# An fp32 encoder layer on one Trainium2 core: attention packed into fewer ticks, operand sets built earlier, and a reordered beginning

## The chip, the cores and the metric

The kernel runs on one core of a Trainium2 chip. The metric is the device time of one launch in microseconds (us), as the median of several runs. One more execution was recorded by the hardware profiler. TensorE is PE in its rows (PEld: its weight loads), VectorE is DVE, ScalarE is ACT, GpSimd is POOL and SyncE is SP.

## The reference

One layer over 768 tokens (a prompt of 256 and a sample of 512 are two segments that share the weights), all in float32:

```python
ada = jax.nn.silu(c) @ w_ada + b_ada
shift, scl, gate = jnp.split(ada, 3, axis=-1)
h = _rms(x, norm_g) * (1 + scl[:, None, :]) + shift[:, None, :]
proj = h @ w_in                                   # 2048 -> 10240
pool_u, pool_z, q, k, v, attn_z, g_pool, g_attn = jnp.split(proj, cuts, axis=-1)
pool_y = _pool_mixer(pool_u, pool_w, pool_scale) * jax.nn.silu(pool_z)
...                                               # q and k are normalised per head
attn_y = _neighbourhood_attention(q, k, v, rpb) * jax.nn.silu(attn_z)
merged = jax.nn.sigmoid(g_pool) * (pool_y @ w_pool_up) + jax.nn.sigmoid(g_attn) * (attn_y @ w_attn_up)
return x + gate[:, None, :] * (merged @ w_o)
```

Attention has 16 heads of 64 channels; each token attends to a window of up to 8 rows of 16 columns on a grid 64 wide, with a learned position bias.

## The kernel before

Every engine's instructions are written out in order by one generator (`steps`), so an engine waits wherever its next instruction is not ready. Activations lie as channels x tokens, 128 channels by 768 tokens in two halves of 384 (`TH`). Each large product is made of float32 split into a high and a low fp32r part, three matmuls of 128 x 128 by 384 columns for one block.

The matrix products come in sets, one per left operand: XA (channels 0 to 1023 of the normalised input, against w_in), XB (channels 1024 to 2047), XR (the pooled branch, against w_pool_up), XY (the attended branch, against w_attn_up), MA and MB (the halves of the merged branches, against w_o). Each set has an *opening* of two plain units (96 matmuls, L458) and then *pair jobs* (L440): two blocks of output at a time, by a Strassen-like scheme with seven products over four pairs of channels, 84 matmuls. The program counts in *ticks*: six matmuls each, 14 to a job, 16 to an opening. ScalarE and VectorE split the weights (`whi` at L329, `wlo` at L330) and combine the products (L368 copies one to `u` or `p`).

A set's operands are B11, B12, B21, B22 and the differences T1 to T4, each for four pairs. `Set.put` makes one: ScalarE casts the high part (L194), VectorE subtracts it for the low part (L198); the differences are formed at L218 to L230. `build` lists this work as tasks: fetch a pair (two loads of 384 KB), put its four blocks, make its T's. `whole=n` finishes the first n pairs, T's and all, before the next pair is fetched; the other pairs get their T's after all blocks. `pump` does at most one task in a tick, in an opening one each tick, in pair jobs one every second or third, and only if the buffers not in use exceed the task's need by `spare` (`SLOTS` is 45). When PE comes to an operand that is not there, `need` does all tasks up to it at once, in haste:

```python
def need(st, op, j):
    hurry["on"] = True
    while (op, j) not in st.ops:
        ...
        tasks.pop(0)[2]()
```

Beginning. SP loads 16 tiles of the input (`xin`), five tiles of the modulation weights (`adaw`, five buffers), four units of w_in (`wraw`), then the other `adaw`. ScalarE squares each `xin` tile, VectorE adds the squares (L1031), PE sums them over channels (`ss`, L1036). Then come the modulation's multiplications (`adaacc`, L477) in four groups of 16 steps, with opening ticks of XA in between (first main matmul: L458).

Attention is spread over XB's jobs, one job's matmuls between its pieces: `attention(p, start, pace)` puts unit u's stages at ticks start + pace x u + d. Of a unit's stages on PE, the scores `s` (L568) come at d = 0, the transposes `vt` of V (L607) at 5, the transposes `pt` of the probabilities (L629) at 9, the products `op` with V (L662) at 13. `vt` and `pt` share one PSUM tag; VectorE frees it by writing the low part `pl` (L647). `n2` (the norms of q and k, L503) and `yk` (L539) come once a head. Each head takes the time of 56 ticks: four jobs.

The branch gates are loaded ahead by `sig_load`.

Of the kernel before, what the change touches and what calls it, by code (L numbers as in the profile page):

```python
# [51 lines left out]
def encoder_layer(ctx: ExitStack, tc: tile.TileContext, xT, cT, w_ada2, w_ada4, b_ada, norm_g, w_in, pool_w,  # L52
# [22 lines left out]
    def free(n=1):  # L75
        heap["live"] -= n
# [219 lines left out]
    st_ = {"ahead": 3, "loaded": 0, "split": 0, "raw_live": 0}  # L296
# [190 lines left out]
    def norms(p, start):  # L487
# [11 lines left out]
        def sums():  # L499
            n2 = ps_aux.tile([P, 512], F32, tag="pt", name="n2")  # L500
# [267 lines left out]
    def store_part(f):  # L768
        def go(i, t):
            pool.dma_start(part_d[f], flat(t))  # L770
            after(3, free)
        return go

    def merge_part(f):
        def go(i, t):
            pool.dma_start(part_d[f], flat(t), accum_op=ALU.add)
            after(3, free)
        return go
# [82 lines left out]
    GR = (3, 2, 1, 0)  # L861

# [16 lines left out]
    for p in range(8):  # L879
# [20 lines left out]
    def pu_done(f):  # L900
        def go(i, t):
# [5 lines left out]
            sig_load(f + 4)  # L907
        return go

    def au_done(f):  # L910
        def go(i, t):
# [3 lines left out]
            if 16 + f + 4 < 32:  # L915
                sig_load(16 + f + 4)
# [84 lines left out]
    with tc.tile_pool(name="start", bufs=1) as sp_:  # L1001
# [21 lines left out]
        load_more()  # L1023
        acc = slot("sumsq")
        for kt in range(KT):
            if kt == 0:
                act.activation(flat(acc), flat(xin[kt]), AF.Square)
            else:
                sq = slot("sq0")
                act.activation(flat(sq), flat(xin[kt]), AF.Square)  # L1030
                dve.tensor_tensor(flat(acc), flat(acc), flat(sq), op=ALU.add)  # L1031
                free()
        free(8)
        ss = ps_aux.tile([P, 2, 512], F32, tag="s", name="ss")
        for h in range(2):
            pe.matmul(ss[:, h, :TH], ones, acc[:, h, :], start=True, stop=True)  # L1036
# [28 lines left out]
        for g, (inner, tail) in enumerate(PLAN):  # L1065
            adaw["acc"] = ps_aux.tile([P, 512], F32, tag="pt", name="adaacc")
            done = 0
            for kt in range(KT):
                ada_mm(adaw["acc"], kt, adaw[g, kt // 2][:, 512 * (kt % 2) : 512 * (kt % 2) + 512])
                if kt % 2:  # L1070
                    load_ada()
# [6 lines left out]
            if g == 0:  # L1078
                prepare(3)
# [9 lines left out]
        ready = {"pairs": 0}  # L1089
# [18 lines left out]
        def late_out(g):  # L1108
            tr = turned(4)
            if g < 2:  # L1110
                modulation(4 + g, tr)
                ready["pairs"] = 2 * g + 2
# [24 lines left out]
        early = started + 14 * len(jobsA) - 100  # L1137
        heap["spare"] = 4
        build(XB, x_pair, lambda j: j < ready["pairs"] and clock["now"] >= early, x_make, 0, 1)
        run(14 * len(jobsA))  # L1140


    with tc.tile_pool(name="mixp", bufs=1, reuse_waits="tile") as mp_:
# [5 lines left out]
        run(1)  # L1149
        free()  # L1150
        run(16 + 8 * 14 + 4 * 4 - 1)
# [23 lines left out]
    with tc.tile_pool(name="attn", bufs=1, reuse_waits="tile") as at_:  # L1175
        state["pool"] = at_
        act.preload_act_table_set(LNEXP)
        now = clock["now"]
        for p in range(8):
            attention(p, now + 56 * p + 25, 8)  # L1180
        run(31 * 14 - 40)
        build(XR, pooled)
        build(XY, attended, lambda j: state.get("attended", -1) >= 2 * j + 1, gated, 2, 1)
        run(40)
        for f in range(4):
            sig_load(f)
        run(16 + 2 * 14)
# [98 lines left out]
```

## Time and profile before

| | us |
|---|---|
| median of 3 runs | 2068.19 |
| lowest and highest | 2067.04, 2069.83 |
| the profiled execution | 2067.87 |
| its span in the trace | 2066.1 |
| PE busy, of the span | 1949.3 |
| DVE, ACT, POOL busy | 1332.6, 1025.3, 259.6 |

The profiled execution is the time of the launch in which the trace was taken; the span is what the trace covers of it. Busy times of engines overlap. A busy PE need not be at full speed: the clock granted to it stands beside it in the views by stretch, 1.00 for the higher of its two levels.

### The profile page before, as it was taken

The numbers are of one execution on the slowest core, as the hardware profiler recorded it, in microseconds if no ns is written. First come the engines' busy times: TensorE is split into PE (matmuls) and PEld (weight loads), VectorE is DVE, ScalarE is ACT, GpSimd is POOL, SyncE is SP. The second block draws the span as 40 slices with busy tenths as digits, with TensorE's granted clock in tenths as the row PEclk, the third lists the DMA queues.
The fourth block names the chain that finished last, engine by engine and source line by source line (L and its number), as shares of the span: only waits on it lengthen the run. The fifth ranks groups of instructions, "written<-read, shape, count | busy, mean of one in ns | idle before, by whom it ended". The sixth has DMA issues, their size and how long they took to land.

```text
span 2066.1 us, 31567 instructions
## 1 busy us (share of the span) xinstructions
PE 1949.3 (94%) x11812; PEld 1834.4 (89%) x11812; DVE 1332.6 (64%) x2392; ACT 1025.3 (50%) x2207; POOL 259.6 (13%) x385
## 2 busy tenths in 40 slices
PE   3899999999999989999999999999979979999998
PEld 2889898888999879999999999999968968999997
DVE  5755555555566777756667666666766767677654
ACT  4433333333344344546556556556656555456653
POOL 0000000000000045410000100101100001112111
PEclk9999999999999989999999999999979999999999
DMA  9755555553333425555545545445634647767765
GB/s 354 258 189 182 200 189 202 191 189 138 136 138 134 154 57 143 133 126 119 126 97 127 119 105 127 109 115 125 172 119 151 246 157 191 226 162 197 207 174 142
DMA packets 100362, 331.92 MB, mean 161 GB/s; under 512 B 13169, under 2 KB 18289, under 8 KB 100209
## 3 DMA queue, kind: packets, MB, share of 16 engines
q1 hardware_dynamic: 68256, 217.35, 30.9%
q0 software_dynamic: 30944, 112.48, 23.4%
q8 instruction: 92, 1.51, 0.3%
q14 instruction: 62, 0.50, 0.1%
q10 hardware_dynamic: 1008, 0.09, 0.0%
HBM read 251.22 MB, written 78.64 MB: 160 GB/s over the span
## 4 chain that ended last, share of the span: by engine, by line
PE 81%; DVE 6%; ACT 5%; DMA 4%; issue 3%; POOL 0%; SPq 0%; ACTq 0%; POOLq 0%; DVEq 0%
PE acc L440 71%; PE acc L458 2%; PE adaacc L477 2%; PE op L662 1%; DMA adaw<-in_w_ada_dram 1%; DVE wlo L330 1%; ACT whi L329 1%; PE s L568 1%; PE n L503 1%; PE pt L629 1%; DMA wraw<-in_w_in_dram 1%; DVE sumsq L1031 1%; PE yk L539 1%; DMA in<-pooled_d 0%; DMA in<-merged_d 0%
## 5 line engine op out<-in xcount | busy, mean ns | idle before, releaser
L330 DVE TENSOR_TENSOR wlo<-wraw,whi 128x512 fp32r<-128x512 f32 (+1 forms) x357 | 249.1, 699 | 296.6 <-ACT whi L329 283.7
L330 DVE TENSOR_TENSOR wlo<-wsum,whi 128x512 fp32r<-128x512 f32 x420 | 293.6, 699 | 132.5 <-ACT whi L329 130.9
L440 PE MATMUL acc<-xbT,whi 128*128 128x384 f32 x1248 | 339.9, 353 | 10.5 <-DVE xbT L198 5.2
L329 ACT CAST whi<-wsum 128x512 fp32r<-128x512 f32 x420 | 260.6, 621 | 160.0 <-ACT whi L329 49.5
L440 PE MATMUL acc<-xaT,whi 128*128 128x384 f32 x1216 | 313.7, 338 | 1.1 <-ACT u L368 0.6
L329 ACT CAST whi<-wraw 128x512 fp32r<-128x512 f32 (+1 forms) x357 | 215.8, 605 | 116.1 <-PE acc L440 92.8
L368 ACT COPY u<-acc 128x384 f32<-128x384 f32 x210 | 100.5, 478 | 300.5 <-PE acc L440 300.5
L440 PE MATMUL acc<-xbB,whi 128*128 128x384 f32 x936 | 247.3, 345 | 0.5 <-DVE o L757 0.5
L440 PEld LDWEIGHTS acc<-xbT,whi 128*128 128x128 f32 x1248 | 229.9, 196 | 20.1 <-DVE xbT L198 7.4
L440 PE MATMUL acc<-xaB,whi 128*128 128x384 f32 x912 | 235.4, 339 | 0.0
L440 PEld LDWEIGHTS acc<-xaT,whi 128*128 128x128 f32 x1216 | 217.6, 188 | 16.2 <-issue 14.4
L440 PE MATMUL acc<-xbT,wlo 128*128 128x384 f32 x624 | 215.3, 345 | 0.0
L440 PE MATMUL acc<-xaT,wlo 128*128 128x384 f32 x608 | 203.9, 335 | 0.0
L440 PEld LDWEIGHTS acc<-xaB,whi 128*128 128x128 f32 x912 | 163.0, 188 | 11.9 <-issue 9.9
L440 PEld LDWEIGHTS acc<-xbB,whi 128*128 128x128 f32 x936 | 167.4, 191 | 4.4 <-issue 1.4
L440 PE MATMUL acc<-xbB,wlo 128*128 128x384 f32 x468 | 158.1, 338 | 0.0
L353 DVE TENSOR_TENSOR wsum<-wraw 128x512 f32<-128x512 f32 x210 | 145.4, 693 | 13.4 <-DMA wraw<-in_w_in_dram 13.2
L440 PE MATMUL acc<-xaB,wlo 128*128 128x384 f32 x456 | 153.0, 335 | 0.0
L353 DVE TENSOR_TENSOR wsum<-wsum,wraw 128x512 f32<-128x512 f32 x210 | 147.5, 702 | 0.0
L440 PEld LDWEIGHTS acc<-xbT,wlo 128*128 128x128 f32 x624 | 121.8, 195 | 0.0
L440 PEld LDWEIGHTS acc<-xaT,wlo 128*128 128x128 f32 x608 | 114.2, 188 | 0.0
L379 DVE SCALAR_TENSOR_TENSOR o<-u,acc 128x384 f32<-128x384 f32 x105 | 58.2, 554 | 85.8 <-ACT u L368 83.8
(252 smaller groups left out, 3435.9 us busy)
## 6 DMA issues: line engine op xcount, KB each, us to landing
wraw<-in_w_in_dram SPq DMA_DIRECT2D x160, 512.0 KB, 4.4
adaw<-in_w_ada_dram SPq DMA_DIRECT2D x96, 512.0 KB, 5.4
part_d<-o POOLq DMA_DIRECT2D x116, 384.0 KB, 2.8
wraw<-in_w_o_dram SPq DMA_DIRECT2D x32, 512.0 KB, 6.4
o<-part_d POOLq DMA_DIRECT2D x38, 384.0 KB, 4.8
sig<-part_d SPq DMA_DIRECT2D x32, 384.0 KB, 7.0
wraw<-in_w_pu_dram SPq DMA_DIRECT2D x16, 512.0 KB, 4.5
wraw<-in_w_au_dram SPq DMA_DIRECT2D x16, 512.0 KB, 5.9
```

Source lines behind the costliest of these rows:

```text
L329: act.copy(hi[:, :n, :], raw)
L330: dve.tensor_tensor(lo[:, :n, :], raw, hi[:, :n, :].bitcast(F32), op=ALU.subtract)
L353: dve.tensor_tensor(t[:, :n, :], a, b, op=ALU.add)
L368: act.copy(t, c["a"][:, :TH])
L379: dve.scalar_tensor_tensor(c["o2"][:, 1, :], c["u3"], -1.0, c["c"][:, :TH], op0=ALU.mult, op1=ALU.subtract)
L440: pe.matmul(out, w, m, start=s["first"] and j == 0 and k == 0, stop=j == n - 1 and k == 2, skip_group_check=True)
L458: pe.matmul(c["ps"][h], w[:, j, :], mov[h][m], start=s["begin"] and j == 0 and k == 0, stop=last and k == 2, skip_group_check=True)
L477: pe.matmul(acc[32 * j : 32 * (j + 1), :n], cs[:, kt, :], w[:, n * j : n * (j + 1)], start=kt == 0, stop=kt == KT - 1)
L503: pe.matmul(n2[:, 12 * i + 2 * u : 12 * i + 2 * u + 2], flat(c["s" + nm])[:, P * u : P * (u + 1)], blk1[:, 0:P:64], start=True, stop=True)
L539: pe.matmul(c["b"][HALF[h], u // 3, P * (u % 3) : P * (u % 3 + 1)], src, ident, start=True, stop=True)
L568: pe.matmul(s[:, h, :K], a[HALF[h], q0 : q0 + P], b[HALF[h], key0 : key0 + K], start=i == 0, stop=i == 2)
L629: pe.transpose(pt[:n, j, h, :], c["p"][:, h, o_ : o_ + n], ident)
```

## The change

The change has five parts.

1. *Beginning.* The squares of odd `xin` tiles are summed by PE as they come, into the same `ss`; VectorE adds only the even ones. Ten of group 0's 16 modulation steps stand on PE ahead of the last sum. The first three units of w_in load two of their eight channel blocks at first; the rest, and the fourth unit, are loaded after group 0's modulation.
2. *XB's building.* XA's last part writes its outputs into a pool of its own (`outs_a`, seven buffers). XB is built with `whole=2` and `spare` 1, from 110 ticks before the end of XA's jobs instead of 100, and no longer waits for pairs to be modulated.
3. *Attention.* Five heads (`DENSE`) lie over 42 ticks instead of 56, at pace 7 instead of 8; the five jobs that stood in them follow after the last head. `n2` moves from the PSUM tag that `pt` and `vt` share to that of the scores.
4. *XR and XY* are built after attention has ended, with the pool `outs`, XR with `whole=2`. By the program's count XR's opening begins at tick 1142; pair 1 is fetched at 1137, pairs 2 and 3 at 1150. For XY pair 1 is fetched at 1203 (before: 1240), pair 2 at 1240 (1246), pair 3 at 1255 (1259); its T's still come partly in haste. MA's pairs 2 and 3 are fetched four ticks earlier. XB's pairs 2 and 3 are fetched at ticks 555 and 557; its opening begins at 564.
5. *Gates* are loaded two ahead instead of four.

```diff
     def load_more():
-        while st_["loaded"] < len(units) and st_["raw_live"] < RAWBUFS:
+        while st_["loaded"] < min(len(units), st_["upto"]) and st_["raw_live"] < RAWBUFS:
...
-            sp.dma_start(u["tile"][:, : u["n"], :], u["src"])
+            n = 2 if st_["loaded"] < st_["cut"] else u["n"]
+            sp.dma_start(u["tile"][:, :n, :], u["src"][:, :n, :])
...
+    def load_rest():
+        for u in units[: st_["cut"]]:
+            sp.dma_start(u["tile"][:, 2 : u["n"], :], u["src"][:, 2 : u["n"], :])
+        st_["upto"] = len(units)
...
-            n2 = ps_aux.tile([P, 512], F32, tag="pt", name="n2")
+            n2 = ps_aux.tile([P, 2, 512], F32, tag="s", name="n2")[:, 0, :]
...
+    DENSE = 5
...
-        for _ in range(2):
+        for _ in range(1 if p < DENSE else 2):
             a, b = gs.pop(0), gs.pop(0)
             jobs.append((a, b, fill(a), fill(b)))
+    while gs:
+        a, b = gs.pop(0), gs.pop(0)
+        jobs.append((a, b, fill(a), fill(b)))
...
-            sig_load(f + 4)
+            sig_load(f + 2)
...
         for kt in range(KT):
-            if kt == 0:
-                act.activation(flat(acc), flat(xin[kt]), AF.Square)
-            else:
-                sq = slot("sq0")
-                act.activation(flat(sq), flat(xin[kt]), AF.Square)
+            sq = acc if kt == 0 else slot("sq0")
+            act.activation(flat(sq), flat(xin[kt]), AF.Square)
+            if kt % 2:
+                summed(sq, kt == 1, False)
+            elif kt:
                 dve.tensor_tensor(flat(acc), flat(acc), flat(sq), op=ALU.add)
...
-        for h in range(2):
-            pe.matmul(ss[:, h, :TH], ones, acc[:, h, :], start=True, stop=True)
+        EARLY = 2 * ADABUFS
+        for kt in range(EARLY):
+            ada_step(0, kt)
+        summed(acc, False, True)
...
             if g == 0:
+                load_rest()
                 prepare(3)
...
-        early = started + 14 * len(jobsA) - 100
-        heap["spare"] = 4
-        build(XB, x_pair, lambda j: j < ready["pairs"] and clock["now"] >= early, x_make, 0, 1)
-        run(14 * len(jobsA))
+        modulated = 6 + 5 * KT * 4 + 8 * 4 + 6
+        run(modulated)
+
+    with tc.tile_pool(name="outs_a", bufs=1, reuse_waits="tile") as outs["pool"]:
+        early = started + 14 * len(jobsA) - 110
+        heap["spare"] = 1
+        build(XB, x_pair, lambda j: clock["now"] >= early, x_make, 0, 2)
+        run(14 * len(jobsA) - modulated)
+    del outs["pool"]
...
+        first = now + 25
         for p in range(8):
-            attention(p, now + 56 * p + 25, 8)
-        run(31 * 14 - 40)
-        build(XR, pooled)
-        build(XY, attended, lambda j: state.get("attended", -1) >= 2 * j + 1, gated, 2, 1)
...
+            attention(p, first, 7 if p < DENSE else 8)
+            first += 42 if p < DENSE else 56
+        done = first - 56 + 40 + 16 - now
+        run(done)
...
     heap["spare"] = 1
+    build(XR, pooled, whole=2)
+    build(XY, attended, lambda j: True, gated, 2, 1)
+    run(31 * 14 - done)
```

On SP, the loads at the start of the program stood before the change as follows:

```order
L1020 DMA xin<-in_xT_dram 128x768 x16
L1012 DMA adaw<-in_w_ada_dram 128x1024 x5
L307 DMA wraw<-in_w_in_dram 128x1024 x4
L1012 DMA adaw<-in_w_ada_dram 128x1024 x27
L307 DMA wraw<-in_w_in_dram 128x1024 x4
```

and stand now:

```order
L1031 DMA xin<-in_xT_dram 128x768 x16
L1023 DMA adaw<-in_w_ada_dram 128x1024 x5
L308 DMA wraw<-in_w_in_dram 128x256 x3
L1023 DMA adaw<-in_w_ada_dram 128x1024 x8
L315 DMA wraw<-in_w_in_dram 128x768 x3
L308 DMA wraw<-in_w_in_dram 128x1024
L1023 DMA adaw<-in_w_ada_dram 128x1024 x19
L308 DMA wraw<-in_w_in_dram 128x1024 x4
```

The first three `wraw` loads are cut to a quarter, eight `adaw` loads have moved ahead of their rest, and the fourth unit comes after that.

On SP at the end of XB's jobs, the loads of the pooled branch (`pooled_d`, XR's operands, two to a pair) and of w_pool_up (`wraw`) stood as follows, with attention's `bias` in between:

```order
L1160 DMA in<-pooled_d_203 128x768
L1160 DMA in<-pooled_d_204 128x768
L1160 DMA in<-pooled_d_205 128x768
L1160 DMA in<-pooled_d_206 128x768
L561 DMA bias<-in_rpb_dram 128x384
L307 DMA wraw<-in_w_pu_dram 128x1024 x2
L561 DMA bias<-in_rpb_dram 128x512
L307 DMA wraw<-in_w_pu_dram 128x1024 x2
L561 DMA bias<-in_rpb_dram 128x512
L1160 DMA in<-pooled_d_207 128x768
L1160 DMA in<-pooled_d_208 128x768
L307 DMA wraw<-in_w_pu_dram 128x1024
```

and stand now:

```order
L1188 DMA in<-pooled_d_203 128x768
L1188 DMA in<-pooled_d_204 128x768
L308 DMA wraw<-in_w_pu_dram 128x1024 x4
L1188 DMA in<-pooled_d_205 128x768
L1188 DMA in<-pooled_d_206 128x768
L308 DMA wraw<-in_w_pu_dram 128x1024
L904 DMA sig<-part_d_163 128x768
L904 DMA sig<-part_d_164 128x768
L308 DMA wraw<-in_w_pu_dram 128x1024
L1188 DMA in<-pooled_d_207 128x768
L1188 DMA in<-pooled_d_208 128x768
L1188 DMA in<-pooled_d_209 128x768
```

`bias` is gone from here. Pair 1 (`pooled_d_205` and `_206`) has moved behind four weight units, and pairs 2 and 3 (`pooled_d_207` to `_210`, the last one right behind the rows shown) stand together, with two weight units and two `sig` loads between pair 1 and them.

On PE, in a unit of attention (`pt`, `op` and `vt` as above, `xb` the main matmuls of XB), the rows left out being main matmuls, this stood:

```order
L629 MATMUL pt<-ident,p 128x128 x4
L440 MATMUL acc<-xbB_6149,whi 128x384 x2
L440 MATMUL acc<-xbB_6149,wlo 128x384
...
L440 MATMUL acc<-xbT_7169,whi 128x384 x2
L440 MATMUL acc<-xbT_7169,wlo 128x384
L662 MATMUL op<-ph,vh 128x256
L662 MATMUL op<-pl,vh 128x256
L662 MATMUL op<-ph,vl 128x256
L662 MATMUL op<-ph,vh 128x256
L662 MATMUL op<-pl,vh 128x256
L662 MATMUL op<-ph,vl 128x256
L607 MATMUL vt<-ident,o_9480 128x128
```

and now:

```order
L636 MATMUL pt<-ident,p 128x128 x4
L447 MATMUL acc<-xbT_7245,whi 128x384 x2
L447 MATMUL acc<-xbT_7245,wlo 128x384
...
L614 MATMUL vt<-ident,o_9290 128x128
L447 MATMUL acc<-xbT_6103,whi 128x384 x2
L447 MATMUL acc<-xbT_6103,wlo 128x384
L447 MATMUL acc<-xbT_6488,whi 128x384 x2
L447 MATMUL acc<-xbT_6488,wlo 128x384
L669 MATMUL op<-ph,vh 128x256
L669 MATMUL op<-pl,vh 128x256
L669 MATMUL op<-ph,vl 128x256
L669 MATMUL op<-ph,vh 128x256
```

`vt` of the next unit has moved from behind the six matmuls of `op` to a place ahead of them, three ticks behind `pt`, with a tick of main matmuls between it and `op`.

## Rows read from the trace of the kernel before

**Rows 1.** The page's first part: busy us, share of the span, instructions.
```profile
PE 1949.3 (94%) x11812; PEld 1834.4 (89%) x11812; DVE 1332.6 (64%) x2392; ACT 1025.3 (50%) x2207; POOL 259.6 (13%) x385
```

**Rows 2.** Stretches: length, busy (instructions) by engine, PE clock, DMA share, GB/s.
```profile
12.00:52.00 40.00, 20.75 (x286) 14.38 (x287) 26.66 (x47) 15.45 (x25) 0.00 (x0) 0.91 1.02 394
600.00:650.00 50.00, 50.00 (x290) 50.00 (x290) 37.72 (x65) 23.71 (x47) 4.32 (x8) 1.00 0.35 130
700.00:765.00 65.00, 53.18 (x234) 47.54 (x235) 48.51 (x82) 26.99 (x57) 16.75 (x21) 0.82 0.33 81
1156.00:1235.00 79.00, 78.26 (x491) 73.99 (x490) 52.09 (x107) 45.80 (x121) 7.50 (x9) 0.98 0.49 115
1492.00:1568.00 76.00, 59.60 (x270) 50.68 (x269) 47.41 (x96) 42.55 (x102) 2.53 (x4) 0.80 0.33 112
1656.00:1714.00 58.00, 40.60 (x186) 35.17 (x185) 37.77 (x65) 30.58 (x55) 4.01 (x6) 0.89 0.47 152
1796.00:1840.00 44.00, 38.13 (x183) 35.28 (x182) 28.66 (x53) 22.48 (x47) 6.98 (x10) 0.88 0.68 192
1950.00:1974.00 24.00, 22.06 (x126) 21.42 (x125) 13.12 (x24) 14.52 (x30) 4.25 (x6) 1.00 0.51 119
```

**Rows 3.** XR's stretch, main matmuls alone: L440 (pair jobs), then L458 (opening).
```profile
1492.00:1568.00 76.00, 31.08 (x110) 0.80 0.33 112
1492.00:1568.00 76.00, 20.63 (x96) 0.80 0.33 112
```

**Rows 4.** Groups by line in three stretches: xcount, busy, mean ns, idle before, releaser.
```profile
L458 PE MATMUL acc<-xbB,whi 128*128 128x384 f32 x64 | 16.5, 375 | 3.2 <-DVE xbB L198 3.2
L440 PE MATMUL acc<-xbT,whi 128*128 128x384 f32 x44 | 16.1, 432 | 8.3 <-DVE xbT L198 5.2 <-ACT p L368 2.2 <-ACT u L368 0.6
...
L662 PE MATMUL op<-ph,vh 128*128 128x256 f32 (+1 forms) x6 | 2.3, 376 | 4.5 <-ACT ph L642 4.5
...
L458 PE MATMUL acc<-xyB,whi 128*128 128x384 f32 x64 | 16.8, 372 | 5.5 <-ACT xyB L194 3.1 <-DVE xyB L198 2.3
L440 PE MATMUL acc<-xyT,whi 128*128 128x384 f32 x32 | 11.8, 422 | 11.9 <-ACT p L368 6.8 <-DVE xyT L198 4.0 <-ACT xyT L194 0.8
```

**Rows 5.** Timeline of the beginning: start us, duration, instruction [idle before <-releaser].
```profile
0.75 14.74 SPq L1020 DMA_DIRECT2D xin<-in_xT_dram  x16
25.94 2.90 PE L1036 MATMUL ss<-sumsq,ones 128*128 128x384 f32 x4 [25.94 <-DVE sumsq L1031]
29.91 0.33 SPq L1012 DMA_DIRECT2D adaw<-in_w_ada_dram  x1
...
44.60 0.98 PE L458 MATMUL acc<-xaB,whi 128*128 128x384 f32 x4
49.16 0.38 PEld L477 LDWEIGHTS adaacc<-adaw,cs 128*32 128x32 f32 x16 [0.40 <-DMA adaw<-in_w_ada_dram]
```

**Rows 6.** XR's opening: loads with median us to landing, then the timeline.
```profile
in<-pooled_d SPq DMA_DIRECT2D x4, 384.0 KB, 8.9
...
1503.98 0.85 PE L458 MATMUL acc<-xrB,whi 128*128 128x384 f32 x4
1509.57 0.44 PE L458 MATMUL acc<-xrB,whi 128*128 128x384 f32 x1 [1.83 <-DVE xrB L198]
1510.43 1.48 PE L458 MATMUL acc<-xrB,whi 128*128 128x384 f32 x4
```

**Rows 7.** Timeline of two units in one head, and that head's n2 group.
```profile
1187.95 0.60 PE L629 MATMUL pt<-ident,p 128*128 128x128 f32 x4
1191.06 0.68 DVE L647 TENSOR_TENSOR pl<-pt,ph 128x512 fp32r<-128x512 f32 x1
...
1208.89 0.60 PE L629 MATMUL pt<-ident,p 128*96 128x128 f32 x4
1212.38 0.74 DVE L647 TENSOR_TENSOR pl<-pt,ph 96x256 fp32r<-96x256 f32 x2
...
L503 PE MATMUL n<-blk,sq 128*128 128x2 f32 x24 | 3.0, 260 | 0.5 <-DVE vl L622 0.5
```

More of the change, by code (lines that the diff above doesn't have):

```diff
@@ L295, in encoder_layer @@
     units, seq = [], []
-    st_ = {"ahead": 3, "loaded": 0, "split": 0, "raw_live": 0}
+    st_ = {"cut": 3, "upto": 3, "ahead": 3, "loaded": 0, "split": 0, "raw_live": 0}
     def unit(src, uses):
@@ L770, in go @@
             pool.dma_start(part_d[f], flat(t))
-            after(3, free)
+            release(t, 3)
         return go
@@ L776, in go @@
             pool.dma_start(part_d[f], flat(t), accum_op=ALU.add)
-            after(3, free)
+            release(t, 3)
         return go
@@ L914, in go @@
             free()
-            if 16 + f + 4 < 32:
-                sig_load(16 + f + 4)
+            if 16 + f + 2 < 32:
+                sig_load(16 + f + 2)
             def add():
@@ L999, in apply @@
                               op0=ALU.mult, op1=ALU.add)
-    with tc.tile_pool(name="start", bufs=1) as sp_:
+    with tc.tile_pool(name="start", bufs=1, reuse_waits="tile") as sp_:
         ADABUFS = 5
@@ L1023, in encoder_layer, with ada_step, summed @@
         load_more()
+        ss = ps_aux.tile([P, 2, 512], F32, tag="s", name="ss")
         acc = slot("sumsq")
-        for kt in range(KT):
-            if kt == 0:
-                act.activation(flat(acc), flat(xin[kt]), AF.Square)
-            else:
-                sq = slot("sq0")
-                act.activation(flat(sq), flat(xin[kt]), AF.Square)
-                dve.tensor_tensor(flat(acc), flat(acc), flat(sq), op=ALU.add)
-                free()
-        free(8)
-        ss = ps_aux.tile([P, 2, 512], F32, tag="s", name="ss")
-        for h in range(2):
-            pe.matmul(ss[:, h, :TH], ones, acc[:, h, :], start=True, stop=True)
+        adaw["acc"] = ps_aux.tile([P, 512], F32, tag="pt", name="adaacc")
+        def ada_step(g, kt):
+            ada_mm(adaw["acc"], kt, adaw[g, kt // 2][:, 512 * (kt % 2) : 512 * (kt % 2) + 512])
+            if kt % 2:
+                load_ada()
+        def summed(t, first, last):
+            for h in range(2):
+                pe.matmul(ss[:, h, :TH], ones, t[:, h, :], start=first, stop=last)
+        for kt in range(KT):
+            sq = acc if kt == 0 else slot("sq0")
+            act.activation(flat(sq), flat(xin[kt]), AF.Square)
+            if kt % 2:
+                summed(sq, kt == 1, False)
+            elif kt:
+                dve.tensor_tensor(flat(acc), flat(acc), flat(sq), op=ALU.add)
+        EARLY = 2 * ADABUFS
+        for kt in range(EARLY):
+            ada_step(0, kt)
+        summed(acc, False, True)
+        free(KT - 1 + 8)
         rstd, xs = slot("rstd"), slot("xs")
@@ L1065, in encoder_layer @@
         for g, (inner, tail) in enumerate(PLAN):
-            adaw["acc"] = ps_aux.tile([P, 512], F32, tag="pt", name="adaacc")
+            if g:
+                adaw["acc"] = ps_aux.tile([P, 512], F32, tag="pt", name="adaacc")
             done = 0
             for kt in range(KT):
-                ada_mm(adaw["acc"], kt, adaw[g, kt // 2][:, 512 * (kt % 2) : 512 * (kt % 2) + 512])
-                if kt % 2:
-                    load_ada()
+                if g or kt >= EARLY:
+                    ada_step(g, kt)
                 while done < inner * (kt - SKIP) // (KT - 1 - SKIP):
```

15 lines of the change are left out of this document (6 added, 9 removed).

## The prediction

> **What bounds the kernel now.** I read the page's busy shares first [rows 1]: TensorE is busy 1949.3 of 2066.1 us, the next engine, VectorE, 64% of the time. So the time is TensorE's work plus the stretches in which it stands or runs slowly, and those are what an edit can win. Second, I cut the span into stretches by the slices in which PE or its granted clock falls under 9 tenths [rows 2]. An undisturbed stretch, 600 to 650, gives the yardstick: 290 matmuls in 50 us, 172.4 ns each, so a tick of six is 1.034 us. For every other stretch I take its length, less its matmuls at 172.4 ns; what is left I call its loss:
> - XB's opening and first jobs, 700 to 765: 234 matmuls, 40.3 us, loss 24.7.
> - XR's, 1492 to 1568: 110 + 96 main matmuls [rows 3], 35.5 us, and 64 of attention. A head's 79 us stretch, 1156 to 1235, holds 56 ticks, 57.9 us, so its 155 matmuls of attention cost 21.1, 0.136 each; 64 cost 8.7. Loss 31.8.
> - XY's, 1656 to 1714: 186, 32.1 us, loss 25.9.
> - MA's, 1796 to 1840: 183, 31.5 us, loss 12.5.
> - MB's, 1950 to 1974: 126, 21.7 us, loss 2.3. This set has two pairs made whole ahead and an output pool of its own: the best that this kernel shows.
>
> The groups by line say what PE waited for there [rows 4]: nearly all of it for the first use of an operand by an engine that was still making it (VectorE's L198, ScalarE's L194), or for ScalarE's copy of a product (L368). The waits alone are 11.5 of XB's 24.7; the rest is the clock, granted at 0.82, 0.80, 0.89 and 0.88 in the four stretches and 1.00 in the yardstick. So one us of wait taken away gives back up to two.
>
> The beginning is different [rows 5]: until 52 us the DMA engines are full (share 1.02, 394 GB/s) [rows 2]. TensorE does nothing before 25.94, SP can issue the sixth modulation load only at 29.91, when the first has been multiplied, and the first main matmul runs at 44.60. But group 1's last modulation load, waited for at 49.16, stands behind 16.8 MB (16 x 384 KB, 16 x 512 KB, 4 x 512 KB), and those bytes are the same after the change.
>
> **The change, part by part.**
>
> Beginning. Eight of the sixteen squares are summed on TensorE, in order of arrival, not on VectorE. The two `pe.matmul` that make such a sum took 2.90 us from 25.94 [rows 5]; eight at that price, begun at about 10 us, would end at 33; at half of it, if the clock is granted by then, TensorE keeps up with the squares and ends at about 26. Ten modulation steps follow and the norm's last sum after them, so I expect the norm no earlier than before, perhaps 1.3 us later. But modulation no longer waits behind it, its last three loads no longer stand behind 1.7 MB of w_in (4.2 us at 394 GB/s), and the first main matmul can come some 4 us earlier. What decides is the load with 16.8 MB ahead of it, which at most loses a wait for a buffer, about a microsecond. I take 1.5 us, with bounds of +4 (the first matmul's lead kept whole) and -3: three more loads, at the 0.92 us that SP spends on each (14.74 for 16) [rows 5].
>
> That price I weigh against a rule. By the Trainium skill, "DMA: Bandwidth & Descriptors", section "Anatomy of one DMA — SWDGE (gpsimd) path", a transfer has a fixed part of about 2.0 us beside its bytes, which speaks against loading units in parts. Three more at 2.0 would be 6 us, an estimate from that page, and the sum below 2026. The share of 1.02 at 394 GB/s in [rows 2], with loads of 384 and 512 KB, says that such parts overlap here, so I keep 1.5.
>
> XB. Its first two pairs become whole and start ten ticks sooner, into an output pool of seven buffers; both are whole 11 ticks before the opening, pairs 2 and 3 are fetched 9 and 7 ticks before it, and the T's are made before their product. Of its waits [rows 4] those on L198 go (3.2 + 5.2 of 11.5). Those on L368 stay: 2.2 + 0.6, and about as much for the clock: with the small ones the loss after is about 6, gain 18.7. Bounds: 22.4 (as MB), 12.4 (half the loss stays). ScalarE and VectorE do the same work earlier, hidden by XA's last jobs, where 600 to 650 keeps DVE at 75% and ACT at 47% [rows 2].
>
> Attention, XR. Five heads lose 14 ticks of filler each, put back as five jobs after the last head; TensorE's work is equal. Attention ends before XR's building, so neither its matmuls nor their 4.5 us wait on `ph` [rows 4] lie among XR's first jobs. Pair 0 is whole, pair 1 loaded ahead. But pairs 2 and 3 are fetched in the opening's eighth tick, when PE needs them. SP, which by order stands behind only two weight loads and two sig loads there, gets to them about 3.3 us after the opening begins; such loads land in 8.9 us [rows 6]; they are needed 8.3 us after it begins. That is 3.9 us of wait. With 1 us to split them, 2 for the clock and 3 of L368 and T's, the loss after is about 10: gain 22. Bounds: 29.5 (as MB), 5 (clock stays at 0.80 through both phases: 35.5/0.8 - 35.5 = 8.9, with 18 us of waits).
>
> Dense heads. A unit is 7 ticks, so the V transpose of the next unit comes 3 ticks after the transposes of P instead of 4, one tick ahead of `op` instead of behind it. Its PSUM buffer is free when `pl` is written. In two units of a head that is 1213.12 - 1208.89 = 4.23 and 1191.74 - 1187.95 = 3.79 us after the transposes [rows 7]; the transposes and three ticks are 3.4. So two units in a head wait 0.83 and 0.39, 1.2 in all, and 6 for five heads; behind the waiting transpose stand a main tick and `op`. n2 in the other tag gives back up to 0.5 a head (the wait on L622's `vl`) [rows 7], the yk step nearer its scores takes about as much; where a head's lags are shorter, less: I take a loss of 5. Bounds: a gain of 2.5 (only the n2 wait goes), a loss of 25 (0.83 in each of 30 units).
>
> XY. Pair 1 is fetched at tick 1203 instead of 1240, pairs 2 and 3 six and four ticks earlier; the T's come in the same order and haste as before. So the opening's 5.5 us go, and half as much again in clock; the 11.9 us in the T phase stay. Gain 8; bounds 0 and 13.4. MA: everything four ticks (4.1 us) earlier, gain 4, bounds 0 and 10.2 (as MB). Gates two ahead instead of four: a job is 14 ticks, 14.5 us, and a load of this size lands in about 9 [rows 6], so two ahead still cover it, at nothing; if they didn't, ScalarE would wait with the operands behind it, within XY's bounds. MB and the end: nothing moves.
>
> **Sum.** 1.5 + 18.7 + 22 - 5 + 8 + 4 = 49.2. The profiled execution took 2067.87 (span and 1.8 around it), 0.3 under the median: 2067.87 - 49.2 = 2018.7, 2019.
>
> **Rivals.**
> - A, slower: the heads' order. From 54 us gained elsewhere, 1.8 us for each of 30 dense units turns the sign. A wait of 0.83 is not enough, but a fallen clock is: behind a wait of 1.83 in XR's opening four matmuls took 1.48 us that had taken 0.85 [rows 6]; at that price a unit's 42 main matmuls lose 6.6 us. 25 us of waits and a third of the units at that clock would be 91, so about 2105. For it: TensorE takes its queue in order, and ScalarE and VectorE have less time in each unit. Against: the head from 1156 to 1235 has short waits too, and a clock of 0.98 [rows 2].
> - B, the openings keep their haste: loads issued when they are needed land when DMA is full, and the clock stays low. XB 15, XR 12, XY and MA 0, beginning 0, heads -5: 22, so 2046. For it: the late fetch of XR's pairs, and XY's T's, made in the same haste as before. Against: XB's first two pairs are made whole ahead, which is how MB came to a loss of 2.3.
> - C, every opening becomes like MB's, the heads cost nothing: 1.5 + 22.4 + 29.5 + 13.4 + 10.2 + 2.5 = 79.5, so 1988.
> - D, the beginning loses 3 instead of gaining, all else as forecast: 2023.
>
> **Chances.** Forecast 0.53 (own range 2008 to 2032), D 0.05, B 0.24, C 0.12, A 0.05, some 0.01 for a change lost in 4 us. What a measurement of this kernel can tell from no change is 0.2%, 4.1 us. The range goes from 1998 to 2052: it leaves out most of C, A and the worst of B, about 0.2. Faster is everything but A and a little of B: 0.94; same 0.02; slower 0.04.
>
> **What would show it.** Right: 84 to 700 as before; no L198 wait over 1 us in XB's opening and XB's stretch at 46 us for 234 matmuls; dense heads with `vt` waiting for DVE `pl` twice a head, near 65 us from head to head; XR's opening with one wait of about 4 us for `xrB` from DMA `in`; XY's 6.8 us wait for L368 still there. Wrong: a clock under 0.95 in the dense heads; a first steady stretch later than 84 us; long `xrB` or `xyB` waits with DMA full beside them.

## The result and the profile after

The changed kernel takes 2051.29 us (median of 5 runs, 2048.17 to 2054.47), the kernel before beside it 2067.74; the ratio is 0.9916, 95% interval 0.9902 to 0.9929. It is faster by some 16.5 us, where 49 were forecast. Its runs lie further apart than those of before. The profiled execution took 2048.17, the fastest of the five and 3.1 under their median, so what the traces show between the two kernels, 19.8 us, is more than the 16.5 of the medians. Its span is shown in the first lines of the page:

```profile
span 2046.3 us, 31634 instructions
PE 1947.4 (95%) x11844; PEld 1831.9 (90%) x11844; DVE 1322.7 (65%) x2384; ACT 1022.9 (50%) x2207; POOL 260.6 (13%) x385
```

Busy TensorE is 1.9 us less, the span 19.8 less, but this does not mean that only waiting went. Cut where XA's pair jobs begin, first before the change and then after it:

```profile
0.00:97.47 97.47, 60.89 (x712) 49.67 (x713) 66.94 (x135) 42.82 (x80) 3.69 (x16) 0.96 0.83 301
97.47:2066.10 1968.63, 1888.38 (x11101) 1784.76 (x11100) 1265.64 (x2257) 982.48 (x2127) 255.95 (x369) 0.97 0.53 154
...
0.00:103.21 103.21, 76.72 (x744) 57.62 (x745) 59.14 (x127) 42.71 (x80) 3.69 (x16) 0.90 0.79 284
103.21:2046.30 1943.09, 1870.70 (x11101) 1774.24 (x11100) 1263.52 (x2257) 980.21 (x2127) 256.93 (x369) 0.98 0.54 156
```

In the beginning TensorE is busy 15.8 us longer, with the sums of squares and at a lower mean clock, and the part takes 5.7 us more. Behind it the same 11101 matmuls take 25.5 us less: 17.7 less of busy time, most of it the clock's (95.5 us of busy time lay at its lower level before, 65.8 after), and 7.9 less of idle time. The same stretches as [rows 2], each moved to where its set now begins:

```profile
12.00:52.00 40.00, 28.26 (x270) 15.58 (x269) 18.68 (x32) 14.46 (x23) 0.00 (x0) 0.81 1.00 381
706.00:771.00 65.00, 54.29 (x288) 51.98 (x289) 52.15 (x78) 29.09 (x59) 25.51 (x30) 0.95 0.35 95
1500.00:1576.00 76.00, 63.36 (x328) 60.83 (x328) 54.08 (x95) 43.84 (x77) 4.15 (x7) 0.91 0.50 172
1642.00:1700.00 58.00, 42.65 (x195) 38.95 (x194) 38.27 (x65) 30.58 (x54) 4.54 (x7) 0.82 0.47 152
1784.00:1828.00 44.00, 41.53 (x222) 40.70 (x221) 31.46 (x57) 24.77 (x52) 6.42 (x9) 0.92 0.73 213
1932.00:1956.00 24.00, 22.06 (x126) 21.42 (x125) 13.84 (x23) 13.85 (x28) 4.71 (x7) 1.00 0.57 130
```

The clock is back to 0.95 in XB's stretch and 0.91 in XR's, but 0.82 in XY's (0.89 before). What TensorE waited for in three of them and, last, for `vt` in a dense head (groups by line, columns as in [rows 4]):

```profile
L465 PE MATMUL acc<-xbB,whi 128*128 128x384 f32 x64 | 15.3, 357 | 2.3 <-DVE xbB L198 2.3
L447 PE MATMUL acc<-xbT,whi 128*128 128x384 f32 x64 | 18.0, 360 | 8.3 <-ACT u L375 5.6 <-ACT p L375 2.3 <-DVE xbT L198 0.4
...
L465 PE MATMUL acc<-xrB,whi 128*128 128x384 f32 x64 | 15.8, 371 | 4.7 <-ACT xrB L194 4.7
L447 PE MATMUL acc<-xrT,whi 128*128 128x384 f32 x88 | 24.6, 358 | 8.0 <-ACT p L375 4.2 <-ACT u L375 2.5 <-DVE xrT L198 1.2
...
L465 PE MATMUL acc<-xyB,whi 128*128 128x384 f32 x64 | 16.1, 372 | 3.3 <-DVE xyB L198 3.3
L447 PE MATMUL acc<-xyT,whi 128*128 128x384 f32 x33 | 12.3, 423 | 12.0 <-ACT p L375 6.8 <-DVE xyT L198 4.2 <-ACT xyT L194 0.8
...
L614 PE MATMUL vt<-ident,o 128*128 128x128 f32 (+2 forms) x8 | 1.9, 277 | 0.5 <-DVE pl L654 0.3 <-PE acc L447 0.2
```

Set beside [rows 4], this is the main reading. XB's first jobs waited 8.3 us before and wait 8.3 us now (all of it lies in the first job, the same 84 matmuls in both traces); the releaser changed, from VectorE's L198 for the most part to ScalarE's copies of products (L375, L368 before). XY's wait 12.0 instead of 11.9. Two openings improved: XB's from 3.2 to 2.3, XY's from 5.5 to 3.3.

And yet XB's stretch gained. Reckoned as in the prediction, it lost 24.7 us before, 11.5 of them waits; it now loses 15.4 (65 less 288 matmuls), 10.6 of them waits. So 0.9 us of the gain is waiting and 8.5 the clock: the trace has it at the lower level for 23.9 us of this stretch before and for 6.8 after. Before, it fell three times, each within 1.0 us of the end of a wait, of 1.8, 2.2 and 3.5 us; after, it fell twice, behind waits of 1.8 and 5.0, and not behind one of 2.3. Why the same sum of waits cost less clock stays open.

The loss of a stretch (its time less 172.4 ns for each matmul), taken from the starts of single matmuls so that every stretch holds the same work, shows where the 19.8 us came from. One as an example: XR's opening in the changed kernel runs from its first matmul at 1500.01 to the first of its pair jobs at 1524.18, 24.17 us for 96 matmuls, 16.55 us; loss 7.6.

```profile
1500.01 0.85 PE L465 MATMUL acc<-xrB,whi 128*128 128x384 f32 x4
...
1512.90 3.87 ACT L194 CAST xrB<-in 128x384 fp32r<-128x384 f32 x8 [3.19 <-DMA in<-pooled_d]
...
1513.46 1.35 PEld L465 LDWEIGHTS acc<-xrB,whi 128*128 128x128 f32 x4 [4.97 <-ACT xrB L194]
...
1524.18 0.51 PE L447 MATMUL acc<-xrB,whi 128*128 128x384 f32 x2
```

| loss, us | before | after | dense heads only | XR as before | 8 dense | XY 2 whole | together, ahead |
|---|---|---|---|---|---|---|---|
| XB opening, 3 jobs | 31.6 | 21.0 | 32.1 | 21.7 | 20.6 | 21.5 | 19.2 |
| XR opening | 11.1 | 7.6 | 0.1 | 0.1 | 1.6 | 1.5 | 0.1 |
| XR jobs | 35.0 | 16.5 | 15.5 | 21.0 | 16.8 | 20.1 | 12.5 |
| XY opening | 9.1 | 6.6 | 8.8 | 6.5 | 6.3 | 6.1 | 8.4 |
| XY jobs | 26.0 | 26.6 | 26.4 | 26.6 | 26.2 | 12.6 | 8.9 |
| MA | 7.9 | 4.0 | 8.3 | 4.0 | 4.2 | 8.0 | 8.0 |

The columns are the kernels of the experiments below, one execution each; those of "dense heads only" and "XY 2 whole" took 7.4 and 6.6 us more than their kernels' medians. XR's numbers of before contain attention's 64 matmuls, 8.7 us; XB's row contains 24 matmuls of the pooled branch in every column. The other changes of the span: XA's opening ends 5.7 later, XB's further jobs lose 0.9 more, and the stretch of attention up to XR's opening 12.0 more, since all of attention lies in it now.

### The profile page after: what moved, and what is told of

Its sections match the earlier page's. It is cut to its first block, busy times and chain, and to the rows that moved or that the text cites. A ratio compares the mean times of both kernels' runs of the same rounds, so it can differ in the third digit from the quotient of the medians.

```text
span 2046.3 us, 31634 instructions
## 1 busy us (share of the span) xinstructions
PE 1947.4 (95%) x11844; PEld 1831.9 (90%) x11844; DVE 1322.7 (65%) x2384; ACT 1022.9 (50%) x2207; POOL 260.6 (13%) x385
## 5 line engine op out<-in xcount | busy, mean ns | idle before, releaser
L447 PE MATMUL acc<-xbT,whi 128*128 128x384 f32 x1248 | 335.1, 349 | 12.0 <-ACT u L375 9.3
L375 ACT COPY u<-acc 128x384 f32<-128x384 f32 x210 | 100.4, 478 | 293.6 <-PE acc L447 293.6
L447 PEld LDWEIGHTS acc<-xbT,whi 128*128 128x128 f32 x1248 | 223.3, 192 | 21.2 <-ACT u L375 11.9
L447 PEld LDWEIGHTS acc<-xaB,whi 128*128 128x128 f32 x912 | 162.9, 188 | 11.9 <-issue 9.9
L360 DVE TENSOR_TENSOR wsum<-wraw 128x512 f32<-128x512 f32 x210 | 145.1, 691 | 12.2 <-DMA wraw<-in_w_in_dram 12.1
L360 DVE TENSOR_TENSOR wsum<-wsum,wraw 128x512 f32<-128x512 f32 x210 | 147.7, 703 | 0.2
L389 ACT ACTIVATE o<-acc 128x384 f32<-128x384 f32 x105 | 51.6, 492 | 124.9 <-PE acc L447 124.8
```

The source lines that it names most:

```text
L360: dve.tensor_tensor(t[:, :n, :], a, b, op=ALU.add)
L375: act.copy(t, c["a"][:, :TH])
L389: act.activation(c["o2"][:, 0, :], c["a"][:, :TH], AF.Copy, scale=-1.0)
L447: pe.matmul(out, w, m, start=s["first"] and j == 0 and k == 0, stop=j == n - 1 and k == 2, skip_group_check=True)
```

## The experiments

Kernels of one group ran on one chip beside the kernel before; a ratio is to that kernel's runs there (medians 2066.85, 2069.26, 2066.78 and 2066.33). e5 is the changed kernel again: 2050.20, ratio 0.9914 (0.9901 to 0.9928).

> The changed kernel once more, beside the next three on the same chip. Both theories: 2051, with single runs several us to either side, since the runs of the kernels with dense heads lie up to 9 us from their median.

**The beginning: e1, e2, e3, e13.** e1 puts the old beginning into the changed kernel, e2 only its loading, e3 only its sums; e13 puts the new beginning into the kernel before.

```diff
# e1, e2
-    st_ = {"cut": 3, "upto": 3, "ahead": 3, ...
+    st_ = {"cut": 0, "upto": 10 ** 6, "ahead": 3, ...
# e1, e3
-            if kt % 2:
-                summed(sq, kt == 1, False)
-            elif kt:
+            if kt:
                 dve.tensor_tensor(flat(acc), flat(acc), flat(sq), op=ALU.add)
-        EARLY = 2 * ADABUFS
+        EARLY = 0
```

> The changed kernel with the beginning of before (all squares added on VectorE, w_in's units loaded whole, modulation behind the norm's sum), everything else as changed. Theory 1, the beginning's loss stays in the time: the trace shows XA's pair jobs starting at 103.2 instead of 97.5, so this gives back 5.7 us: 2045.5. Rival, the loss is made up later, because loads that come with it lie earlier against the jobs: no more than 1 us, 2050 to 2051.

> The changed kernel with w_in's units loaded whole at the start, ahead of group 0's last modulation loads; the sums on TensorE stay. Theory 1, the parts cost the time (between the landings at 41.0 and 49.4 us 2.2 MB took 8.4 us instead of 5.4, and group 1's last loads land 2.8 us later than before): XA's pair jobs start within 1.5 us of before's 97.5, time 2046 to 2047. Rival, the later norm costs it (its last sum ends 2.4 us later than before, behind ten modulation steps): the start stays at 100 to 103, time 2049 to 2051.

> The changed kernel with all squares added on VectorE and modulation behind the norm's sum, as before; w_in's units still in parts. Theory 1, the parts cost the time: no better than the changed kernel, and some 3 us worse, since the sixth modulation load can be issued only near 30 us, when the queue has run dry (parts landed by 30.3): 2051 to 2055. Rival, the sums and steps on TensorE cost it: 2046 to 2048.

> The kernel before with the new beginning as its only change. Theory 1, the new beginning costs time, because group 1's last modulation loads land about 3 us later and TensorE runs at the lower clock until 52 us: 2069 to 2073, 2 to 6 us over before. Rival, the difference in the first traces is scatter of the loads: within 1.5 us of before.

Measured: e1 2046.91, ratio 0.9905 (0.9885 to 0.9924); e2 2046.20, 0.9906 (0.9892 to 0.9921); e3 2048.86, 0.9919 (0.9902 to 0.9936); e13 2069.44, 1.0010 (1.0001 to 1.0020). The first three cannot be told from the changed kernel, their intervals overlap, so they don't separate parts from sums. e13's interval just leaves out no change: by it the new beginning costs 0.2 to 4 us. The traces agree in the sign, and show that the 5.7 us of the main pair holds scatter: XA's opening ends at 97.5 to 100.4 in the three with the old beginning (before, e1, e4), at 100.7 to 104.5 in the nine with the new one, 2.8 later in the mean. The place where the changed kernel's trace loses it:

```profile
29.73 1.56 PE L1047 MATMUL ss<-sumsq,ones 128*128 128x384 f32 x4
40.85 1.42 PE L465 MATMUL acc<-xaB,whi 128*128 128x384 f32 x3
...
49.47 1.08 PE L484 MATMUL adaacc<-adaw,cs 128*32 128x128 f32 x16 [4.45 <-DMA adaw<-in_w_ada_dram]
```

The norm's last sum stands behind ten modulation steps and starts at 29.73, not 25.94 [rows 5]. The first main matmul comes 3.75 us earlier. But the load of group 1 that is used at 49.47 is its sixth, and two more follow, where before the eighth was there at 49.16: TensorE has the matmuls earlier and then stands 4.45 us for data. No buffer holds these loads back: group 1's last one is issued at 39.77, before the change at 43.45, and lands at 51.96 instead of 49.12. The time goes between the landings of the 13th and the 14th `adaw` load, 40.99 and 49.43, where the rest of the units lands: 2.2 MB in 8.4 us, for which 5.4 would do at the 1.27 us that loads of 512 KB take just before. (e5 takes 7.6 there, e13 7.3.) Why these loads take longer stays open, and neither the loading nor the sums was shown by a time to be the cause by itself.

**Dense heads alone: e4.** In the kernel before, together with `n2` in the tag of the scores:

```diff
+    DENSE = 5
-        for _ in range(2):
+        for _ in range(1 if p < DENSE else 2):
...
-            attention(p, now + 56 * p + 25, 8)
+            attention(p, first, 7 if p < DENSE else 8)
+            first += 42 if p < DENSE else 56
```

> The kernel before, with attention's five dense heads and n2 in the other tag as the only change. Theory 1: a dense head costs 1 us (65.1 us from head to head, less 43.4 of main matmuls, against 78.6 less 57.9), five heads 5 us, and attention no longer in XR's opening gives back its waits of 4.9 us there and some clock: 2062 to 2067. Rival, dense heads are free and their loss in the trace belongs to the jobs moved: 2055 to 2060. Rival, XR's haste stays as it is and only the loss remains: 2072.

Measured: 2051.30, ratio 0.9935 (0.9921 to 0.9949). All three expectations are missed on the low side: one part of the change is worth nearly what the whole is. Its XR rows, over the whole run:

```profile
L458 PE MATMUL acc<-xrB,whi 128*128 128x384 f32 x64 | 13.7, 334 | 0.0
L440 PE MATMUL acc<-xrT,whi 128*128 128x384 f32 x224 | 60.2, 348 | 9.0 <-ACT p L368 5.7 <-DVE xrT L198 2.1 <-ACT u L368 0.7
```

XR's opening, built as before, waits for nothing once attention has ended ahead of it (3.4 us in the kernel before), and 30 us of loss go from XR; 8.7 of them are attention's work, and attention's stretch loses 13.5 more.

**XR and its building: e6, e7, e9.** e6 builds XR and XY as before in the changed kernel, e7 makes one pair of XR whole ahead, e9 has eight dense heads.

```diff
# e6
+        run(31 * 14 - 40)
+        build(XR, pooled)
+        build(XY, attended, lambda j: state.get("attended", -1) >= 2 * j + 1, gated, 2, 1)
# e7
-    build(XR, pooled, whole=2)
+    build(XR, pooled, whole=1)
# e9
-    DENSE = 5
+    DENSE = 8
-        done = first - 56 + 40 + 16 - now
+        done = first - 42 + 40 + 16 - now
```

> The changed kernel, but XR and XY are built as before: from tick 394 on, all blocks ahead of the T's, no pair made whole first, no output pool until XR's first jobs. Theory 1, the new building of XR loses what the early end of attention won: with dense heads alone XR's opening and jobs lose 15.6 us beyond their matmuls, in the changed kernel 24.2; so about 8 us come back: 2043. Rival, the loss in the changed kernel comes from its fuller buffers and its place against the other stages, not from the building: 2050 to 2053.

> The changed kernel with one pair of XR made whole ahead instead of two, so that pairs 2 and 3 are fetched before pair 1's T's. Theory 1, the late fetch costs the wait of 4.65 us in XR's opening and its clock: XR's opening loses 0 to 1 us instead of 7.6, and the time is 2044 to 2046. Rival, T's of pair 1 are then late in the first jobs and the wait only moves there: 2050 to 2052.

> The changed kernel with all eight heads dense, so attention ends 28 ticks earlier and XR's building starts at tick 1084 instead of 1112; pairs 2 and 3 are fetched at 1139 and 1141, and no operand of XR is made in haste any more. Theory 1, XR loses because its operands are made too late (about 25 us beyond its matmuls in the changed kernel, its first loads and blocks in haste): XR loses 5 to 10 us, the time is 2031 to 2037. Rival, dense heads cost and the last three heads pay for it, or the waits for ScalarE's copies of products stay however early the operands are: 2046 to 2050.

Measured: e6 2044.84, ratio 0.9891 (0.9875 to 0.9906); e7 2052.98, 0.9925 (0.9904 to 0.9945); e9 2051.86, 0.9929 (0.9912 to 0.9945). e6 came within 2 us of what was expected: its XR opening loses 0.1 instead of 7.6, its jobs lose more, 21.0 instead of 16.5, so of the new building nothing is left as a gain (the interval overlaps that of the changed kernel). e6 shows one thing more: its XY is built by the code of before, and yet pair 3 is loaded 2.8 us behind the start of XY's opening, as in the changed kernel (5.9 before), and XY's opening and MA lose 6.5 and 4.0, as there. e4, which has neither the new building nor the new loading of the gates, loses 8.8 and 8.3 there. e1 and e10, without the new beginning and without XB's new building, lose 6.3 and 6.6, 4.3 and 4.0. So what XY and MA gained does not come from the new building. By the program the gates are the likely cause: a loaded gate holds a buffer, `pump` fetches only when enough buffers are free, and two ahead leave more than four. No run takes the gates alone, so this is argued, not shown. e7 went the rival's way: the opening waits 1.7 us, the first jobs 6.8 for L375. e9's opening loses 1.6, and yet the time did not move: the jobs still wait, and the stretch of attention takes 8.5 us more than in e5.

```profile
L465 PE MATMUL acc<-xrB,whi 128*128 128x384 f32 x64 | 14.3, 339 | 0.8 <-DVE xrB L198 0.8
L447 PE MATMUL acc<-xrT,whi 128*128 128x384 f32 x224 | 59.0, 344 | 12.1 <-ACT p L375 7.2 <-ACT u L375 3.2 <-DVE xrT L198 1.6
```

No operand of XR is made in haste here, and TensorE waits 7.2 us for one copy. So haste was not the whole cause.

**XB: e10, e8.** e10 builds XB as before. e8 leaves out three of the four levels of pooling sums for the group of window 16, so its output lacks them.

```diff
# e10
+        early = started + 14 * len(jobsA) - 100
+        heap["spare"] = 4
+        build(XB, x_pair, lambda j: j < ready["pairs"] and clock["now"] >= early, x_make, 0, 1)
# e8
-        chores.extend((2, lambda lev=lev: level(lev)) for lev in range(g + 1))
+        chores.extend((2, lambda lev=lev: level(lev)) for lev in range(g + 1 if f < 6 else 1))
```

> The changed kernel with XB built as before (from 100 ticks ahead, one pair whole, spare 4, no output pool in XA's last part). Theory 1: the traces show XB's opening and first two jobs losing 31.6 us before and 21.0 in the changed kernel, so this gives 10 us away: 2060. Rival, the gain there is lost again by a later weight load and XB's first jobs lose the same either way: 2050 to 2053.

> The changed kernel with three of the four levels of the pooling sums left out for the group of window 16 (both of its channel blocks), so the work of GpSimd beside XB's first job is less. Theory 1, VectorE's instructions take 1.3 to 2.4 us instead of 0.55 to 0.69 while GpSimd sums (738 to 745 in the changed kernel), which delays a weight buffer, its load, ScalarE's queue and then TensorE by 4.97 us at 750: that wait goes or shrinks under 1.5 us, XB's first two jobs lose 9 to 12 us instead of 16.7, time 2044 to 2047. Rival, the weight load is late by itself (its buffers, SP's order): the wait stays, 2050 to 2052.

Measured: e10 2061.99, ratio 0.9969 (0.9956 to 0.9981); e8 2048.51, 0.9903 (0.9889 to 0.9918). e10 puts XB's building at some 11 us (the ratio differs by 0.0055 from e5's), as its trace says (XB's opening and first jobs lose 33.1, in e5's 20.3). In e8 the wait before the second job fell from 4.44 (e5) to 2.59, not under 1.5, and the time is not apart from the changed kernel's: the mechanism has a part in that wait, no more. It reads so in the changed kernel's timeline:

```profile
739.09 5.78 POOL L719 TENSOR_TENSOR sum<-sum 128x797 f32<-128x797 f32 x3
739.48 1.86 DVE L230 SCALAR_TENSOR_TENSOR xb<-xb 128x384 f32<-128x384 f32 x1
741.27 1.86 DVE L198 TENSOR_TENSOR xbT<-xb,xbT 128x384 fp32r<-128x384 f32 x1
...
743.05 2.37 DVE L360 TENSOR_TENSOR wsum<-wsum,wraw 128x512 f32<-128x512 f32 x1
...
745.50 0.89 SPq L308 DMA_DIRECT2D wraw<-in_w_in_dram  x2
749.13 0.62 ACT L336 CAST whi<-wraw 128x512 fp32r<-128x512 f32 x1 [3.00 <-DMA wraw<-in_w_in_dram]
749.65 0.47 ACT L375 COPY u<-acc 128x384 f32<-128x384 f32 x1
750.17 0.37 PEld L447 LDWEIGHTS acc<-xbT,whi 128*128 128x128 f32 x2 [5.29 <-ACT u L375]
```

While GpSimd sums (L719), VectorE's instructions take 1.86 and 2.37 us, so the last use of a weight buffer (L360) ends 4.9 us late (1.3 + 1.3 + 1.7 here and 0.6 ahead of it), the next load is issued at 745.50, and ScalarE stands before that weight with the copy `u` behind it.

**XY, and the copies: e11, e12, e14, e15, e16.** e11 is eight dense heads with whole units; e12 adds two whole pairs of XY. e14 is the changed kernel with VectorE's difference of each T issued one task ahead of ScalarE's cast of it. e15 puts together what gained or seemed to (whole units, XR as in e6, XY as in e12, five dense heads); e16 is e15 with the edit of e14.

```diff
# e12, e15, e16
-    build(XY, attended, lambda j: True, gated, 2, 1)
+    build(XY, attended, lambda j: True, gated, 2, 2)
# e14, e16: differences() gives a part for VectorE and a part that puts
+        def turns(seq):
+            for k, (j, n) in enumerate(seq):
+                def go(k=k, j=j, n=n):
+                    if k == 0:
+                        diff(j, n)[0]()
+                    if k + 1 < len(seq):
+                        flush()
+                        diff(*seq[k + 1])[0]()
+                    diff(j, n)[1]()
+                tasks.append((1, lambda: True, go))
```

> Eight dense heads and w_in's units loaded whole at the start, the rest as changed. Theory 1, the two add up (the second gave about 4 us by itself): 2027 to 2033. Rival, the units in parts cost nothing that can be measured: the same as eight dense heads alone, within 2 us.

> As the run before, and XY built with two pairs whole ahead of the others instead of one: then no operand of XY is made in haste either (pairs 2 and 3 fetched at ticks 1249 and 1251 instead of 1240 and 1255, pair 1's blocks no longer behind pair 2's fetch). Theory 1, haste is what costs: XY loses 33 us beyond its matmuls in the kernel before and in the changed one, and would lose 8 to 15; 2008 to 2016. Rival, XY's waits come from the loads of the attended branch and its gating, whatever the order: 2025 to 2033.

> The changed kernel with VectorE's differences of an operand issued one task ahead of ScalarE's cast of it, for every T of every set but XA's; no work more or less. Theory 1, ScalarE stands in its queue before a cast until VectorE has the difference (1.8 to 2.1 us each, four to six in a row at 1528 to 1538 with eight dense heads), with the copy of a product behind it, and TensorE waits up to 7.2 us for that copy: the waits for L375 after XR's and XY's openings shrink by half, their first two jobs lose 5 to 9 us less together, time 2041 to 2046. Rival, VectorE has too much to do there, so it is late with the low parts instead: waits move from L375 to L198, 2049 to 2053.

> The changed kernel with five dense heads, w_in's units loaded whole, XR built as before and XY with two pairs whole: the parts that gained. Theory 1, they add: 2051 less 4 (units), less 6 (XR), less 12 (XY): 2027 to 2033. Rival, XR's building runs later into XY's and takes its gain back: 2037 to 2042.

> The run before with the differences issued a task ahead of the casts too. Theory 1: 3 to 8 us under the run before. Rival, no difference or slower, as VectorE is late instead.

Measured: e11 2049.23, ratio 0.9914 (0.9901 to 0.9926); e12 2037.37, 0.9858 (0.9837 to 0.9879), 12 us under e11; e14 2039.44, 0.9871 (0.9857 to 0.9885), some 9 us under e5 by the ratios; e15 2033.96, 0.9847 (0.9832 to 0.9862); e16 2017.72, 0.9765 (0.9750 to 0.9780), 16 us under e15 and the fastest kernel of the study. Most expectations missed: e11 by 16 us, and it is 2.6 from eight dense heads alone where its rival said 2; e12 lies above both of its ranges; e14 gained more than expected, e16 twice the most expected; e15 fell between its theory and its rival, and its XR jobs lose 25.5, more than in any column of the table but the first. XY in e12, over the whole run:

```profile
L465 PE MATMUL acc<-xyB,whi 128*128 128x384 f32 x64 | 16.6, 377 | 2.3 <-DVE xyB L198 2.3
L447 PE MATMUL acc<-xyT,whi 128*128 128x384 f32 x224 | 59.2, 344 | 8.3 <-ACT p L375 4.2 <-ACT u L375 3.4 <-DVE xyT L198 0.8
```

and the first jobs of XR and XY in e16 (waits of the changed kernel over the whole run: 10.3 and 16.3):

```profile
L456 PE MATMUL acc<-xrT,whi 128*128 128x384 f32 x224 | 59.1, 344 | 6.5 <-ACT p L384 3.7 <-DVE xrT L198 1.8 <-ACT u L384 0.8
L456 PE MATMUL acc<-xyT,whi 128*128 128x384 f32 x224 | 59.0, 343 | 5.3 <-ACT p L384 4.2 <-ACT u L384 0.6 <-DVE xyT L198 0.5
```

Why the order of a difference and its cast matters is to be seen in XY's first job in the changed kernel:

```profile
1673.23 0.55 DVE L222 TENSOR_TENSOR in<-in 128x384 f32<-128x384 f32 x1
1673.81 0.56 DVE L223 SCALAR_TENSOR_TENSOR in<-in 128x384 f32<-128x384 f32 x1
1674.40 0.51 ACT L194 CAST xyT<-in 128x384 fp32r<-128x384 f32 x1 [2.08 <-DVE in L223]
...
1676.66 0.56 DVE L223 SCALAR_TENSOR_TENSOR in<-in 128x384 f32<-128x384 f32 x1
1677.25 0.51 ACT L194 CAST xyT<-in 128x384 fp32r<-128x384 f32 x1 [1.82 <-DVE in L223]
1677.67 0.47 ACT L375 COPY p<-acc 128x384 f32<-128x384 f32 x1
...
1678.20 1.01 PE L447 MATMUL acc<-xyT,whi 128*128 128x384 f32 x2 [6.78 <-ACT p L375]
```

TensorE has finished a product and needs its bank; the copy (L375) stands in ScalarE's queue behind casts of XY's T's, each of which waits 1.8 to 2.1 us for a difference that VectorE makes in between other work. e14 moved no work, only that order. In XY's first jobs the wait for L375 fell from 6.8 to 4.4 there, in XR's it stayed at 4.2; all of XY's jobs lose 16.0 (25.3 in e5), MB's first 1.0 (2.7), and MA gives 5.2 back. So the mechanism is shown, by e14 for XY and again by e16 against e15, where XR's jobs lose 12.5 instead of 25.5; how much of each remaining wait it makes is not.

## Why the prediction was wrong

The direction was right, the size three times too large. That 2051.29 lies inside the range, 0.7 us from its end, is luck, since most terms missed. It is nearest to rival B's 2046, but B's reason holds only in part: XR's late loads cost what B feared, while the clock rose in XB and XR; rival D's loss in the beginning came too. Term by term, from the two traces:

- *Beginning*, +1.5 forecast: a loss of 5.7 in the traces, of 0.2 to 4 by e13. The step that failed is "at most loses a wait for a buffer": the bytes ahead of group 1's last load are the same, but it landed 2.8 us later although it was issued 3.7 us earlier; the bytes took longer. By the Trainium skill, "DMA: Bandwidth & Descriptors", section "Anatomy of one DMA — SWDGE (gpsimd) path", three more loads would lose 6, which is the prediction's 2026, an estimate; that section is on loads issued by GpSimd, these are SP's, and e13's interval ends at 4.
- *XB*, 18.7 forecast: 9.7 in the traces (31.6 less 21.0 and 0.9), some 11 by e10. Of the 8.4 us of L198 waits 5.7 went; one of 1.8 stayed in the opening. The step that failed is "Those on L368 stay": they grew from 2.8 to 7.9 us, in place of what was removed. The clock's part fell from 13.2 to 4.7, not to the 2.8 forecast.
- *XR*, 22 forecast, and *dense heads*, -5: together 10.0 (the fall in XR's two rows, less 12.0). The wait for the late loads was forecast as 3.9 and is 4.7, with its place right. The failed step is to credit the gain to the new building: e4 has it from the early end of attention alone, and e6 shows no gain by the building. "3 of L368 and T's" is 8.0 in the jobs, and "2 for the clock" 6.8: XR's stretch loses 19.5 (76 less 328 matmuls), not 10, with 12.7 of waits.
- The heads themselves: `vt` waits 0.3 for `pl`, not 1.2 a head, and attention's stretch and XR's share of it come to about the same before (156.1 + 8.7, and 4.5 of waiting in [rows 4], 169.3 us) and after (168.0). The loss of 5 did not come. The three further heads of e9 did cost 8.5; why these and not the first five stays open.
- *XY*, 8 forecast: 1.9. The opening's waits fell by 2.2, not 5.5: pair 3's two loads still land in the opening, 8.1 and 9.6 us behind its start (12.9 and 13.9 before). *MA*, 4 forecast: 3.9. By e6 neither comes from the new building that the prediction named; the gates, which it put "at nothing", are the likely source. *MB*: nothing moved, as forecast.

Behind XB and XR stands one step, that a wait taken away is gone: "one us of wait taken away gives back up to two" was applied to waits that came back at another line. A wait by line is the last of several engines' lags. The first jobs of a set need ScalarE for casts and for copies of products, in one queue; with the operand on time, TensorE waits for the copy, which stands behind a late weight's cast in XB and behind T's casts in XY. The rate itself did not hold either: XB's stretch gave back 9.3 us for 0.9 of waiting. Rival A didn't come: the clock in the heads stayed near that of before.

## What to carry to other kernels

When a wait on an operand is removed, look up what else stands in the queue of the engine that made it, above all what frees TensorE's banks, and price that as the next wait; e14 shows that order alone can be worth 9 us. Count the clock's share of a loss apart from the waits: here it fell where the waits did not. Ending one stage before the next one's operands are needed (e4) gave most of what the whole change gave. Where a step has two causes in it, run each part alone in the quiet kernel: here the old kernel scattered less than the new one, and only there could some 2 us be told from nothing, and just so.

## What was not expected of the hardware

VectorE's 128x384 subtraction takes 0.55 us, and 1.86 where GpSimd sums beside it; its 128x512 addition 0.68, and 2.37. It was so in the kernel before too. The Trainium skill, "SBUF — State Buffer", section "SBUF: two separate sides", says that VectorE with two inputs from SBUF and GpSimd exclude each other on a shared pair of ports, one waiting out the other's whole instruction; the trace agrees: in each kernel 17 such instructions take over 1.2 us, and each lies beside a sum of GpSimd's that takes 1.5 to 2.3 us, while six that read a product (`acc`) beside such a sum take 0.54 to 0.62, no longer than alone. Four others that read SBUF alone beside one stayed short too.
